# A feed-forward's second product by seven in two blocks, and a second buffer for the weights that a DMA splits

## The chip, the cores and the metric

The kernel runs on one core of a Trainium2 chip. The metric is device time in microseconds (us), from three runs of the kernel before: 2097.94, 2100.37 and 2103.01, median 2100.37. Beside these there is one profiled execution, from which all rows below are read. Engines are named as the profile names them: PE is the matmul engine and PEld its weight loads, DVE the vector engine, ACT the scalar engine, POOL GpSimd, SP the engine whose queue issues most of the transfers.

## The reference

One layer of an encoder, in float32, on 256 tokens of width 2048, with 256 memory tokens and a feed-forward width of 5632.

```python
def swiglu_ffn(h, w_in, w_out):
    gate, up = jnp.split(h @ w_in, 2, axis=-1)
    return (jax.nn.silu(gate) * up) @ w_out

x = x + 0.5 * swiglu_ffn(rms_norm(x, ffn1_norm), ffn1_w_in, ffn1_w_out)   # first feed-forward
h = rms_norm(x, mix_norm)
p = h @ w_mix_in                                   # conv value | conv gate | u | v
ya = silu(layer_norm(depthwise_conv31(val * sigmoid(gate))))
yb = gelu(u) * (masked w_s @ layer_norm(gelu(v)) + b_s)
x = x + concat(rms_norm(ya), rms_norm(yb)) @ w_mix_out
x = x + memory_cross_attention(rms_norm(x), rms_norm(mem))
x = x + 0.5 * swiglu_ffn(rms_norm(x), ffn2_w_in, ffn2_w_out)              # second feed-forward
return rms_norm(x, final_norm)
```

The change touches the second product (`@ w_out`) of the first feed-forward, the start of the mixer (`h @ w_mix_in`) and the first product (`@ w_in`) of the second feed-forward.

## The kernel before, in words

**Numbers in two parts.** A float32 operand is kept as a rounded part ("hi") and the remainder ("lo"). A product is three matmuls: hi by hi, hi by lo, lo by hi, all summed in PSUM. Weights come by DMA as raw tiles of 128x1024 float32 (512 KB); ACT writes hi (a cast), DVE writes lo (a subtraction). In `gemm_n` that is L115 and L116, in a feed-forward's groups L372 and L373 (`parts`). Four raw buffers are shared by the whole kernel (`wraw`), and three for the split ones (`whl`).

**A feed-forward's first product** goes over eleven groups of 512 columns of gate and up each (`group`; group 0 is in `run`). A group goes over the 16 k tiles of 128 rows in eight pairs, in the order SCSCSCCC. A pair C ("eight") is plain: two k tiles x two halves of the tokens x gate and up x three matmuls, 24 matmuls of 128x512 (`by_two`). A pair S ("seven") is done by a scheme with seven products in the place of eight, 21 matmuls (`three`): DVE first makes sums of weight blocks (L422, L423, L428, L435), and the matching sums of the token side ("forms") are made once, beforehand (`sides`). The seven products lie in all eight PSUM banks: six of the pool `ps` ("acc") and both of `pa` ("aux"). After the last S the banks of the products 1, 5, 6 and 7 are joined in SBUF, and at the group's end the banks of 2, 3, 4 and 8 are added (L492).

**Sums by DMA.** Three k tiles of each group (2, 7 and 13; two in the last) don't go through DVE. `summed` loads the raw tile, ACT writes minus hi into the place of lo and hi into its own, and a DMA issued by POOL adds the raw weights onto it (L394). The result lies in `hl_s`; the first feed-forward has a second such buffer in a place that comes free after group 0 (`x_given`), the second feed-forward has one. `summed` for the next use is issued after the matmuls of the present one.

**A feed-forward's second product** needs the result h with the features in the partitions. `turning` makes four transposes on PE into an aux bank, and the sink splits it (L123, L124). Each of the 22 turns gives two of the 44 k tiles; four turns are done in the last group. The product itself is four calls of `gemm_n`, one for each 512 output columns: 22 steps of two k tiles, 12 matmuls each, two banks. The other 18 turns are put one behind each step of the first call. The result is copied, turned back and added to x (`joins`), which also makes the mixer's input `x_hl` and its sums of squares.

**The mixer** begins with four calls of `gemm_n` on `w_mix_vg`. Two turns of the feed-forward's last block are done in the first of them. The convolution's steps wait in a list (`later`) from which `beside` takes a budgeted amount at each step of `gemm_n`. Its result `y_hl` is needed for `w_mix_out`.

**Order.** The instruction order on each engine is made by the framework's scheduler, which simulates the program as written and allots buffers and banks as they come free; each engine's queue is then in order.

## Time and profile before

| | us |
|---|---|
| median of three runs (2097.94 to 2103.01) | 2100.37 |
| the profiled execution | 2096.62 |
| its span, first to last instruction | 2094.9 |

| Engine | busy us | share of the span | instructions |
|---|---|---|---|
| PE | 2082.5 | 99% | 9786 |
| PEld | 1741.6 | 83% | 9786 |
| DVE | 1577.4 | 75% | 2217 |
| ACT | 1165.2 | 56% | 1451 |
| POOL | 67.7 | 3% | 83 |

The granted clock of PE is 0.999 of full speed over the span, that is 2.4 GHz. Matmuls are pipelined and their ends are modelled, so one matmul's duration (some 390 ns for 128x512) is not the pace at which they follow one another; that pace is read from the starts. A window's line gives the busy time of each engine in it, with the number of its instructions.

### The profile page before, as it was taken

To read this page: it belongs to the slowest core of one execution; us is meant where nothing else is said; L and a number is where in the kernel's file an instruction comes from. 1 tells how busy PE (TensorE), PEld (TensorE's weight loads), DVE (VectorE), ACT (ScalarE), POOL (GpSimd) and SP (SyncE) were. 2 spreads that over 40 slices of the span, in tenths; PEclk is the share of its full clock that TensorE was granted. 3 is DMA by queue.
4 is the path that set the end of the run, shared out by engine and by line. 5 is a ranking of instruction groups with operands and counts; after the bars stand their busy time and mean duration, and the time that the engine had idled before them with its cause. 6 is when DMAs were issued, how large, how long until landed. Compare 5 with 4: busy or idle time off the path is not lost.

```text
span 2094.9 us, 26646 instructions
## 1 busy us (share of the span) xinstructions
PE 2082.5 (99%) x9786; PEld 1741.6 (83%) x9786; DVE 1577.4 (75%) x2217; ACT 1165.2 (56%) x1451; POOL 67.7 (3%) x83
## 2 busy tenths in 40 slices
PE   9999999999999999999999999999999999999998
PEld 7888888888888888888888898888888888888886
DVE  7888888875655589888877666778888888787754
ACT  8665666554544454445665454556665666554443
POOL 0000000000000000000000000000000000000000
PEclk9999999999999999999999999999999999999999
DMA  9787778755665666555555543576777777556664
GB/s 368 241 263 246 226 228 263 228 183 169 226 189 188 216 233 198 187 180 183 182 197 188 186 157 117 200 272 218 217 248 251 241 225 246 182 163 203 195 192 152
DMA packets 122387, 442.34 MB, mean 211 GB/s; under 512 B 13584, under 2 KB 13968, under 8 KB 121872
## 3 DMA queue, kind: packets, MB, share of 16 engines
q1 hardware_dynamic: 113040, 407.08, 57.0%
q0 software_dynamic: 8640, 32.51, 8.3%
q8 instruction: 76, 1.25, 0.2%
q10 hardware_dynamic: 576, 1.06, 0.1%
q14 instruction: 55, 0.45, 0.1%
HBM read 438.49 MB, written 2.10 MB: 210 GB/s over the span
## 4 chain that ended last, share of the span: by engine, by line
PE 96%; DMA 2%; issue 1%; ACT 1%; DVE 0%; POOL 0%; SPq 0%; DVEq 0%; ACTq 0%; POOLq 0%
PE acc L192 12%; PE acc L191 12%; PE acc L190 12%; PE acc L319 9%; PE acc L321 9%; PE acc L318 9%; PE acc L144 8%; PE acc L151 4%; PE acc L307 3%; PE acc L305 3%; PE acc L306 3%; PE aux L293 1%; PE aux L307 1%; PE aux L305 1%; PE aux L306 1%
## 5 line engine op out<-in xcount | busy, mean ns | idle before, releaser
L116 DVE TENSOR_TENSOR hl<-raw,hl 128x1024 fp32r<-128x1024 f32 (+1 forms) x402 | 488.5, 1216 | 277.3 <-ACT hl L115 276.3
L115 ACT CAST hl<-raw 128x1024 fp32r<-128x1024 f32 (+1 forms) x402 | 419.6, 1045 | 477.8 <-PE acc L192 291.0
L373 DVE TENSOR_TENSOR hl<-spare,hl 128x1024 fp32r<-128x1024 f32 (+1 forms) x128 | 146.6, 1149 | 34.0 <-ACT hl L372 31.0
L372 ACT CAST hl<-spare 128x1024 fp32r<-128x1024 f32 (+1 forms) x128 | 126.2, 994 | 69.4 <-PE acc L321 25.9
L319 PE MATMUL acc<-hl,x_hl 128*128 128x512 f32 x408 | 147.7, 391 | 0.3 <-DVE hl L124 0.2
L373 DVE TENSOR_TENSOR hl<-raw,hl 128x1024 fp32r<-128x1024 f32 (+1 forms) x107 | 120.7, 1131 | 29.7 <-ACT hl L372 28.3
L372 ACT CAST hl<-raw 128x1024 fp32r<-128x1024 f32 (+1 forms) x107 | 103.5, 979 | 69.6 <-PE acc L321 26.7
L318 PE MATMUL acc<-hl,x_hl 128*128 128x512 f32 x408 | 141.8, 390 | 0.3 <-ACT hl L123 0.3
L321 PE MATMUL acc<-hl,x_hl 128*128 128x512 f32 x408 | 126.5, 389 | 0.0
L372 ACT CAST ring<-spare 128x1024 fp32r<-128x1024 f32 (+1 forms) x81 | 80.4, 997 | 58.9 <-PE acc L321 19.0
L373 DVE TENSOR_TENSOR ring<-spare,ring 128x1024 fp32r<-128x1024 f32 (+1 forms) x81 | 93.0, 1153 | 13.9 <-ACT ring L372 12.6
L191 PE MATMUL acc<-hl,m_hl 128*128 128x512 f32 x256 | 100.3, 392 | 0.0
L191 PE MATMUL acc<-hl,x_hl 128*128 128x512 f32 x256 | 100.3, 392 | 0.0
L192 PE MATMUL acc<-hl,m_hl 128*128 128x512 f32 x256 | 100.2, 391 | 0.0
L192 PE MATMUL acc<-hl,x_hl 128*128 128x512 f32 x256 | 99.8, 390 | 0.0
L319 PE MATMUL acc<-ring,x_hl 128*128 128x512 f32 x248 | 91.4, 389 | 0.0
L190 PE MATMUL acc<-hl,m_hl 128*128 128x512 f32 x256 | 91.2, 392 | 0.0
L318 PEld LDWEIGHTS acc<-hl,x_hl 128*128 128x128 f32 x408 | 76.4, 188 | 16.6 <-ACT hl L123 0.5
L319 PEld LDWEIGHTS acc<-hl,x_hl 128*128 128x128 f32 x408 | 76.2, 188 | 16.8 <-DVE hl L373 0.8
L190 PE MATMUL acc<-hl,x_hl 128*128 128x512 f32 x256 | 90.0, 391 | 0.0
L321 PEld LDWEIGHTS acc<-hl,x_hl 128*128 128x128 f32 x408 | 76.6, 188 | 16.0
L318 PE MATMUL acc<-ring,x_hl 128*128 128x512 f32 x248 | 88.8, 389 | 0.0
(362 smaller groups left out, 4974.9 us busy)
## 6 DMA issues: line engine op xcount, KB each, us to landing
spare<-in_ffn_w_in SPq DMA_DIRECT2D x195, 512.0 KB, 7.0
raw<-in_ffn_w_out SPq DMA_DIRECT2D x176, 512.0 KB, 3.5
raw<-in_ffn_w_in SPq DMA_DIRECT2D x156, 512.0 KB, 6.4
hl_s<-in_ffn_w_in POOLq DMA_DIRECT2D x44, 512.0 KB, 8.8
raw<-in_w_mix_vg SPq DMA_DIRECT2D x32, 512.0 KB, 4.5
raw<-in_w_k SPq DMA_DIRECT2D x32, 512.0 KB, 3.6
raw<-in_w_v SPq DMA_DIRECT2D x32, 512.0 KB, 4.3
raw<-in_w_mix_out SPq DMA_DIRECT2D x32, 512.0 KB, 4.6
```

Source lines behind the costliest of these rows:

```text
L115: nc.scalar.copy(out=hl[:, 0, :size], in_=raw[:, :size])
L116: newest[0] = nc.vector.tensor_tensor(out=hl[:, 1, :size], in0=raw[:, :size], in1=hl[:, 0, :size].bitcast(F32), op=ALU.subtract)
L144: nc.tensor.matmul(acc, lhsT=hi[:, k], rhs=xs[k], start=first and k == 0, stop=last and k == kk - 1, skip_group_check=True,)
L151: nc.tensor.matmul(acc[:, 0], lhsT=lo[:, k], rhs=xs[k][:, 0], start=False, stop=last and k == kk - 1, skip_group_check=True,)
L190: nc.tensor.matmul(acc[t], lhsT=x[:, 0, s], rhs=hi[:, k], start=k0 + k == 0, stop=False)
L191: nc.tensor.matmul(acc[t], lhsT=x[:, 0, s], rhs=lo[:, k], start=False, stop=False)
L192: nc.tensor.matmul(acc[t], lhsT=x[:, 1, s], rhs=hi[:, k], start=False, stop=k0 + k == nk - 1)
L318: nc.tensor.matmul(acc[t][g], lhsT=x[:, 0, s], rhs=hi[:, cols[g]], start=(t, g) in first, stop=False)
L319: nc.tensor.matmul(acc[t][g], lhsT=x[:, 0, s], rhs=lo[:, cols[g]], start=False, stop=False)
L321: nc.tensor.matmul(acc[t][g], lhsT=x[:, 1, s], rhs=hi[:, cols[g]], start=False, stop=last)
L372: self.cast = nc.scalar.copy(out=hl[:, 0, :n], in_=raw[:, :n])
L373: newest[0] = nc.vector.tensor_tensor(out=hl[:, 1, :n], in0=raw[:, :n], in1=hl[:, 0, :n].bitcast(F32), op=ALU.subtract)
```

## The change

The second product of the first feed-forward goes over two blocks of 1024 columns (`out_block`) in the place of four of 512. In each, four of the 22 pairs of k tiles (9, 12, 15 and 18) go by seven, the others plain. The first block takes the pairs in order, the second begins with 9 and takes the four early. A block uses four acc banks, and while its pairs by seven last all eight. The 18 turns are spread over the first block's first seven pairs, three a pair at first; the turns of the four pairs also make the sums of the token side (`out_sides`). The raw weights have four buffers, and two more from the seventh pair on; the split ones five. The weights are laid out anew, so that a k tile of 1024 columns is one row of 4 KB in each partition, as before.

Four turns of the result are left for the mixer. Its first two products are therefore begun together: the first halves (k tiles 0 to 7) of both, with the turns at every second step, and then the second halves.

The second feed-forward gets a second buffer for sums by DMA (`pair`). It lies where the results of the last two groups (h9, h10) will be, and its raw tile where h8 will be. Up to group 7 the uses alternate between the two buffers; from group 8 on there is one.

```diff
+OUT_S = (9, 12, 15, 18)
+OUT_STEPS = (
+    list(range(KF // 2)),
+    [9, 0, 1, 12, 2, 3, 15, 4, 5, 18, 6, 7, 8, 10, 11, 13, 14, 16, 17, 19, 20, 21],
+)
...
-    def gemm_n(w, x_hl, per=0.0, between=None, after=4):
-        acc = [ps.tile([P, 2, 256], F32, name="acc").rearrange("p a b -> p (a b)") for _ in range(2)]
+    def gemm_n(w, x_hl, per=0.0, between=None, after=4, acc=None, ks=None, step=2):
+        acc = acc or [ps.tile([P, 2, 256], F32, name="acc").rearrange("p a b -> p (a b)") for _ in range(2)]
         nk = w.shape[1]
-        for k0 in range(0, nk, 2):
+        for k0 in ks or range(0, nk, 2):
...
-            if between and k0 >= after:
+            if between and k0 >= after and k0 % step == 0:
...
+            self.high_pool, self.pair = high, pair
+            if pair:
+                second = high.tile([P, 2, 1024], F32R, name="hl_s2", tag="pair")
+                self.h += [high.tile([P, 2, G], F32, name="h8"), None, None]
+                high.tile([P, 120], F32, name="to_512")
+            else:
+                self.h += [high.tile([P, 2, G], F32, name=f"h{j}") for j in range(8, NG)]
...
+            if pair:
+                self.hls.append(second)
+                self.raws_summed.append(self.h[8].rearrange("p a b -> p (a b)"))
...
-            nc.sync.dma_start(out=raw, in_=self.w_in[j, :, k])
+            nc.sync.dma_start(out=raw, in_=self.w_in[j, :, k] if j < NG else self.w_out[j - NG, :, k])
             return raw
+        def buffer(self, at):
+            return at % 2 if not self.pair or self.sums_at[at][0] < 8 else 0
+        def following(self, at):
+            same = [i for i in range(at + 1, len(self.sums_at)) if self.buffer(i) == self.buffer(at)]
+            return same[0] if same else None
...
-            raw, hl = self.raws_summed[at % len(self.hls)], self.hls[at % len(self.hls)]
+            raw, hl = self.raws_summed[self.buffer(at)], self.hls[self.buffer(at)]
...
+            form = self.forms[self.spairs.index(p)] if j < NG else self.out_forms[OUT_S.index(p)]
...
+                if between is not None and k % 2 == 1:
+                    between()
...
+        def banks(self, b, names):
+            for name in names:
+                b[name] = bank(pa if name in "67" else ps, "aux" if name in "67" else "acc")
...
+            if self.pair and j == NG - 2:
+                both = self.high_pool.tile([P, 2, 2, G], F32, name="h_pair", tag="pair")
+                self.h[NG - 2:] = [both[:, i] for i in range(2)]
...
+        def out_block(self, n, result, hook, between=None):
+            b = {}
+            self.begun = set()
+            steps = OUT_STEPS[n]
+            for i, p in enumerate(steps):
+                if p in OUT_S:
+                    if "5" not in b:
+                        self.banks(b, "57612348" if i == 0 else "5761")
+                    done = all(q not in OUT_S for q in steps[i + 1:])
+                    self.seven(NG + n, p, b, done)
+                    if done:
+                        o = result()
+                        places = [o[:, t, g * G:(g + 1) * G] for g in range(2) for t in range(2)]
+                        self.joins_sevens(b, *places)
+                else:
+                    if i == 0:
+                        self.banks(b, "2348")
+                    self.eight(NG + n, p, b, i == len(steps) - 1, False, between)
+                hook(i)
+            for acc, i in (("2", 0), ("3", 2), ("4", 1), ("8", 3)):
+                nc.vector.tensor_tensor(out=places[i], in0=places[i], in1=b[acc], op=ALU.add)
+            return o
+        def out_sides(self, form, tp):
+            f1, f2 = ev.tile([P, T], F32, name="tu"), ev.tile([P, T], F32, name="tg")
+            second = ev.tile([P, T], F32, name="sq")
+            nc.scalar.copy(out=second.rearrange("p (k t) -> p k t", k=2), in_=tp[:, :, P:])
+            a11, a21, a12, a22 = tp[:, 0, :P], second[:, :P], tp[:, 1, :P], second[:, P:]
+            f = [f1[:, :P], f1[:, P:], f2[:, :P], f2[:, P:]]
+            nc.vector.scalar_tensor_tensor(out=f[0], in0=a21, scalar=-1.0, in1=a22, op0=ALU.mult, op1=ALU.subtract)
+            nc.vector.scalar_tensor_tensor(out=f[1], in0=f[0], scalar=-1.0, in1=a11, op0=ALU.mult, op1=ALU.subtract)
+            nc.vector.tensor_tensor(out=f[2], in0=a11, in1=a21, op=ALU.subtract)
+            nc.vector.tensor_tensor(out=f[3], in0=a12, in1=f[1], op=ALU.subtract)
+            for i, both in enumerate((f1, f2)):
+                s = slice(2 * i, 2 * i + 2)
+                split(form[:, s, 0], form[:, s, 1], both.rearrange("p (f n) -> p f n", f=2))
...
+            if len(self.hls) > 1:
                 self.summed(1)
...
+                    if self.out_forms is not None and i in OUT_S:
+                        self.out_sides(self.out_forms[OUT_S.index(i)], tp)
...
-        for n in range(4):
-            acc = gemm_n(a["ffn1_w_out"][n], ff.of, per=0.8 if n else 0.0, between=turns, after=0 if n == 0 else 4)
-            if n == 0:
-                pool = stack.enter_context(ff.late)
-                pool = stack.enter_context(tc.tile_pool(name="ffn1", bufs=1, reuse_waits="tile"))
-            o = pool.tile([P, 2, G], F32, name="o", bufs=2)
-            for t in range(2):
-                nc.scalar.copy(out=o[:, t], in_=acc[t])
-            turns += [turning(o, 2 * i * P, joins(4 * n + 2 * i)) for i in range(2)]
-        ff.high.close()
+        ff.ring, ff.raws = [], []
+        def next_turn():
+            if turns:
+                turns.pop(0)()
+        def turns_first(i):
+            if i == 0:
+                more = big.tile([P, 4, 2, 1024], F32R, name="more_out", tag="S2")
+                ff.ring += [more[:, q] for q in range(2)]
+                forms = more[:, 2:].rearrange("p a two n -> p (a two n)")
+                ff.out_forms = [
+                    forms[:, q * 1024:(q + 1) * 1024].rearrange("p (f two n) -> p f two n", two=2, n=P) for q in range(4)
+                ]
+            for _ in range(2 if i < 4 else 1):
+                next_turn()
+            if i == 6:
+                stack.enter_context(ff.late)
+                ff.high.close()
+                pool = rest["pool"] = stack.enter_context(tc.tile_pool(name="ffn1", bufs=1, reuse_waits="tile"))
+                ff.sums = pool.tile([P, 1024], F32, name="sums_out")
+                ff.raws += [pool.tile([P, 1024], F32, name=f"raw_out{q}") for q in range(2)]
+        def result():
+            return rest["pool"].tile([P, 2, 2 * G], F32, name="o", bufs=2)
+        def turned(o, n):
+            return [turning(o, 2 * i * P, joins(8 * n + 2 * i)) for i in range(4)]
+        o = ff.out_block(0, result, turns_first, next_turn)
+        turns += turned(o, 0)
+        def beside_second(i):
+            if i == OUT_STEPS[1].index(OUT_S[-1]):
+                ff.ring = []
+                rest["x_hl"] = gained_tile("S2")
+            elif i > 9:
+                beside(1.4)
+                if i % 2 == 0 and turns:
+                    turns.pop(0)()
+        o = ff.out_block(1, result, beside_second)
+        turns += turned(o, 1)
+        x_hl = rest["x_hl"]
...
+            accs = []
+            for n in range(2):
                 load_gate(n)
                 later.appendleft((1.6, memory_parts(n)))
-                acc = gemm_n(a["w_mix_vg"][n], lambda k: x_hl[:, k], per=1.35, between=turns, after=2)
+                accs.append(gemm_n(
+                    a["w_mix_vg"][n], lambda k: x_hl[:, k], per=1.35, between=turns, after=0, ks=range(0, 8, 2), step=4
+                ))
+            for n in range(NCT // 2):
+                if n < 2:
+                    acc = gemm_n(a["w_mix_vg"][n], lambda k: x_hl[:, k], per=1.35, between=turns, acc=accs[n], ks=range(8, KD, 2))
+                else:
+                    load_gate(n)
+                    later.appendleft((1.6, memory_parts(n)))
+                    acc = gemm_n(a["w_mix_vg"][n], lambda k: x_hl[:, k], per=1.35, between=turns, after=2)
...
+        ff = FeedForward(stack, ("S0", "S1", "S2"), x_hl, lambda k: col("ffn2_norm", k), a["ffn2_w_in"], PATTERNS[1], SUMMED[1], pair=True)
...
-    a["ffn1_w_out"] = _tiled(g["ffn1_w_out"][0], 512)
+    w = g["ffn1_w_out"][0].reshape(KF // 2, 2, P, 2, 2, 512)
+    w = np.stack([w[:, 0, :, :, ::-1], w[:, 1]], axis=1).reshape(KF, P, 2, 1024)
+    a["ffn1_w_out"] = np.ascontiguousarray(w.transpose(2, 1, 0, 3))
```

## Rows read from the trace of the kernel before

**Rows 1.** the page: its span and the busy time of each engine.

```profile
span 2094.9 us, 26646 instructions
PE 2082.5 (99%) x9786; PEld 1741.6 (83%) x9786; DVE 1577.4 (75%) x2217; ACT 1165.2 (56%) x1451; POOL 67.7 (3%) x83
```

**Rows 2.** waits of PE: engine, line, releaser: us in total, times, longest.

```profile
PE acc L319 <- DMA hl_s<-in_ffn_w_in: 0.9, 1, 0.9
```

**Rows 3.** windows (us; busy us and count of each engine; clock; DMA share; GB/s).

```profile
50.00:450.00 400.00, 400.00 (x1768) 331.10 (x1767) 328.54 (x395) 244.95 (x271) 25.48 (x30) 1.00 0.76 237
550.00:715.00 165.00, 165.00 (x739) 136.57 (x738) 86.31 (x97) 76.77 (x95) 0.00 (x0) 1.00 0.61 195
1505.00:1547.00 42.00, 41.06 (x182) 33.67 (x181) 33.66 (x42) 25.21 (x28) 2.63 (x3) 1.00 0.75 232
1547.00:1713.00 166.00, 165.97 (x733) 137.15 (x732) 137.12 (x165) 103.91 (x113) 10.46 (x12) 1.00 0.77 241
1713.00:1822.00 109.00, 109.00 (x482) 89.99 (x481) 89.03 (x106) 66.36 (x72) 6.12 (x7) 1.00 0.71 219
```

**Rows 4.** timeline of PEld (start, us, engine, line, tiles), two steps of `gemm_n`.

```profile
696.16 0.41 PEld L190 LDWEIGHTS acc<-hl,hB 128*128 128x128 f32 x2
...
715.21 0.41 PEld L190 LDWEIGHTS acc<-hl,hC 128*128 128x128 f32 x2
```

**Rows 5.** timeline of PEld in the second feed-forward: its waits for `hl_s`.

```profile
1507.77 0.30 PEld L319 LDWEIGHTS acc<-hl_s,x_hl 128*128 128x128 f32 x2 [1.36 <-DMA hl_s<-in_ffn_w_in]
...
1549.57 0.30 PEld L319 LDWEIGHTS acc<-hl_s,x_hl 128*128 128x128 f32 x2 [0.45 <-DMA hl_s<-in_ffn_w_in]
...
1715.70 0.30 PEld L319 LDWEIGHTS acc<-hl_s,x_hl 128*128 128x128 f32 x2 [0.34 <-DMA hl_s<-in_ffn_w_in]
```

**Rows 6.** DMA issues (count, KB, median us to landing), and landing of `hl_s` (min/median/max).

```profile
raw<-in_ffn_w_out SPq DMA_DIRECT2D x176, 512.0 KB, 3.5
hl_s<-in_ffn_w_in POOLq DMA_DIRECT2D x44, 512.0 KB, 8.8
...
DMA to landing us min/median/max: 5.2/8.8/9.9
```

**Rows 7.** DVE by line (xcount: min/median/max ns; or busy us, mean ns).

```profile
L408 DVE TENSOR_TENSOR spare<-spare x6: 282/284/287, 6.0 to 1384.7; 128x128 f32<-128x128 f32 x6
L422 DVE TENSOR_TENSOR spare<-raw x34: 679/683/695, 41.8 to 1800.2; 128x512 f32<-128x512 f32 x34
L492 DVE TENSOR_TENSOR spare<-spare,acc x80: 676/679/690, 90.4 to 1839.0; 128x512 f32<-128x512 f32 x80
...
L373 DVE TENSOR_TENSOR hl<-raw,hl 128x1024 fp32r<-128x1024 f32 x89 | 108.3, 1220 | 12.3 <-ACT hl L372 10.9
```

**Rows 8.** timeline at a group's end in the second feed-forward (DVE and PE).

```profile
1500.92 2.47 DVE L492 TENSOR_TENSOR spare<-spare,acc 128x512 f32<-128x512 f32 x4
...
1501.68 0.61 PE L321 MATMUL acc<-ring,x_hl 128*128 128x512 f32 x2
...
1502.13 0.39 PE L305 MATMUL acc<-ring 128*128 128x512 f32 x1
```

**Rows 9.** what a turn costs: eight loads (timeline), then DVE by line.

```profile
508.27 1.02 PEld L293 LDWEIGHTS aux<-ident,h 128*128 128x128 f32 x8
...
L124 DVE TENSOR_TENSOR hA<-aux,hA x16: 679/687/692, 460.4 to 1862.3; 128x512 fp32r<-128x512 f32 x16
L637 DVE SCALAR_TENSOR_TENSOR xT<-aux,xT x8: 683/691/692, 541.8 to 726.0; 128x512 f32<-128x512 f32 x8
L269 DVE SCALAR_TENSOR_TENSOR x_hl<-xT,pv,x_hl x48: 472/478/480, 544.1 to 1380.1; 128x256 fp32r<-128x256 f32 x48
```

**Rows 10.** waits of DVE's first sum of a pair (us in total, times, longest).

```profile
DVE spare L422 <- DMA raw<-in_ffn_w_in: 20.0, 11, 2.8
```

**Rows 11.** who writes and first reads `y_hl` (first and last start, us).

```profile
L144 PEld LDWEIGHTS acc<-y_hl,hl x256: 187/188/192, 1080.6 to 1169.5; 128*128 128x128 f32 x128
...
L124 DVE TENSOR_TENSOR y_hl<-tg,y_hl x16: 410/417/419, 1039.3 to 1069.7; 128x256 fp32r<-128x256 f32 x16
```

More of the change, by code (lines that the diff above doesn't have):

```diff
@@ L410, in sides, with x, half, begins @@
             split(self.forms[i][:, :, 0], self.forms[i][:, :, 1], f)
-        def x(self, k, t):
+        def x(self, j, k):
+            return self.x_hl[:, k] if j < NG else self.of(k)
+        def half(self, j, k, t):
             s = slice(t * P, (t + 1) * P)
-            return self.x_hl[:, k, 0, s], self.x_hl[:, k, 1, s]
-        def seven(self, j, p, b, first, last):
+            x = self.x(j, k)
+            return x[:, 0, s], x[:, 1, s]
+        def begins(self, name):
+            first = name not in self.begun
+            self.begun.add(name)
+            return first
+        def seven(self, j, p, b, last):
             k = 2 * p
```

66 lines of the change are left out of this document (32 added, 34 removed).

## The prediction

> **What bounds the kernel now.** I read the page first, for who is busy: PE 99%, beside it weight loads (PEld) 83% and DVE 75% [rows 1]. The ends of matmuls are modelled, so 99% alone does not say that PE is full, and I asked next what PE waits for: outside the launch and the attention stage one wait is left, 0.9 us for `hl_s` [rows 2]. Third come the windows by stage. PEld is busy for 331.10 of 400 us in the first feed-forward's groups and for 136.57 of 165 us in its second product: 82.8% both times, although DVE is at 82% in the one and 52% in the other [rows 3]. So 82.8% is what PEld shows while PE runs through: every product of 128x512 has one load, and they come evenly. Fourth, the period of one product: between the loads at 696.16 and 715.21 lie seven steps of `gemm_n` with 12 products each, 84 products in 19.05 us or 0.2268 us each [rows 4]. The time is a count of products times that, plus the few places where PEld falls under 82.8%. A change gains only by taking away products or such a place, and loses only by making new ones.
>
> **Products taken away.** A pair of k tiles costs the second product 12 products for each of four blocks of 512 columns, 48 in all, and 22 pairs make 1056. Now a plain pair costs 24 for each of two blocks of 1024 columns, again 48; a pair by seven costs 7 x 3 = 21 a block, 42. Four pairs (9, 12, 15, 18) save 6 each: 24 products. The transposes stay as many as they were. At 0.2268 us, and all of it on the path because PE runs through in this stage [rows 3, 4], that is 5.44 us. Bounds: nothing lower is shown, since no row has a product of this shape at another period.
> The Trainium skill (TensorE: Matmul & The Clock Gate, section "Wait — 56ns, not 53.3ns?") puts one product at its columns over 2.4 GHz plus 2.5 ns, 215.7 ns for 512 columns. By that the 24 would give 5.18 us, an estimate from the page; the rows here have 226.8 ns, with a load of its own before each product, and the measurement decides.
>
> **The second buffer for sums.** In the second feed-forward PEld falls under 82.8% in three places, each one a wait for `hl_s`: idle for 1.36, 0.45 and 0.34 us before 1507.77, 1549.57 and 1715.70 [rows 5]. By the windows these cost (34.78 - 33.67) / 0.828 = 1.34, (137.45 - 137.15) / 0.828 = 0.36 and (90.25 - 89.99) / 0.828 = 0.31 us [rows 3]. Each is the first use in a group (k = 2) after the last use in the group before (k = 13). Between the two lie k = 14, 15 and one pair by seven, 45 products or 10.2 us, and the one buffer must in that time be filled by two ACT instructions and then a DMA of 5.2 to 9.9 us [rows 6]. With two buffers in groups 1 to 7 each filling has another use's time more, so the first two waits go: 1.70 us. The third is at the start of group 8, where one buffer is left again; I let it stand. Bounds: 0, if the wait only moves to the two groups with one buffer, and 2.01, if all three go. The first feed-forward has two such buffers and shows 82.8% over 400 us [rows 3], so I take 1.70. The extra load at the start is one transfer on SP's queue and one on POOL's, ahead of need by a group.
>
> **The rhythm by seven.** A pair by seven costs DVE four additions or subtractions of 0.68, three splits of 1.22 and half a split, 0.69 by estimate [rows 7, 9]: 7.07 us in 4.76 us of PE. Two plain pairs follow with 4 x 1.22 = 4.88 us of DVE in 10.88. Together 11.95 of 15.64 us, 76%. The groups run at 82% with PE full [rows 3]: cost 0. The joins add 16 DVE additions of 0.68, 10.9 us, and take eight ACT copies away; they lie in the three plain pairs at a block's end and cost 0 there for the same reason. If that cover were gone, the price is that of the ends of blocks below.
>
> **Turns and sides.** The 18 turns left now fall into the first seven pairs, three a pair at first. Such a pair gives PE 24 x 0.2268 plus 12 transposes of about 0.12 (eight loads in 1.02 us) [rows 9], 6.9 us; DVE has 2 x 1.22 + 3 x 0.69 = 4.5. Four turns also make the sides for their pair on DVE: 4 x 0.28 [rows 7] and two half-width splits of about 0.42, between the 0.28 and the 0.69 of the neighbouring widths, 2.0 us. 6.5 of 6.9: it fits once, not twice in a row. What is scarce is the two aux banks: a side keeps its bank until its last subtraction, and behind a transpose that waits for a bank stand all later products on PE. Bounds: 0, and 4 x 2.0 = 8 us if PE stood for every side.
>
> **The ends of blocks.** The first block needs four banks at once where two did, and two of them are still read by group 10's final additions. At a group's end four such additions take 2.47 us in a row, and the next group's first product starts 0.45 us after the last one of the old [rows 8], that is at the pace of two products. In the first block the second token half is wanted six products, 1.36 us, after the start, when two of four additions are done. The same holds from the first block to the second. Bounds: 0, and 2.47 us for each of the two ends. The new buffers for raw weights lie on h8 to h10, so their transfers wait on SP's queue for the last turn, and the next weight transfers behind them; a transfer takes 3.5 us to land [rows 6] and two k tiles in hand last 5.4, so 0 here.
>
> **Into the mixer.** Four turns are left after the last block instead of two. The first halves of the mixer's first two products, 8 steps or 21.8 us, run before their features are wanted. Until then DVE has four additions (2.7), eight splits (9.8) and, for four turns, 0.69 + 4 x 0.48 each [rows 9], 10.4 us with the squares' additions set at the same 0.48. That is 22.9 us, but the last feature is wanted three steps later still, at 30 us: 0, and a step, 2.7 us, if the first turn came that late. The convolution's first input comes three steps, 8.2 us, later than before; `y_hl` is complete at 1069.7 + 0.4 and first read at 1080.6 [rows 11], so 2.3 us of cover are left: 0.
>
> **The sum.** For sides and ends together I take 1.0 us of new standstill: the ten seams inside the first feed-forward's windows cost 0 [rows 3], the row nearest to the ends, and something is left for what no row shows, four banks wanted at once and a bank held by a side. The profiled execution took 2096.62 us (span 2094.9 and 1.7 around it): 2096.62 - 5.44 - 1.70 + 1.0 = 2090.5, 6.1 less. The median of the runs shown is 2100.37, 3.75 above the profiled one, so I predict 2100.37 - 6.1 = 2094.3.
>
> **Rivals.**
> A. The second buffer brings nothing. The filling hangs on the POOL queue, whose transfers land after 5.2 to 9.9 us [rows 6], and a wait that is late for another reason than the buffer stays. Then 2096.62 - 5.44 + 1.0 = 2092.2, on the median's scale 2095.9. Against it: the first feed-forward's groups use the same queue and lose nothing.
> The Trainium skill (SBUF — State Buffer, the paragraph on the "DVE blocks DMA" trap) says that descriptors of transfers issued by GpSimd are held up while VectorE runs an instruction that takes the port both share. By that rule the landing would follow DVE's load, and the same DVE load stays after the change, which is this rival; the spread from 5.2 to 9.9 us leaves room for it.
> B. The ends and the sides eat the gain: two ends at 2.47 and half of the sides' 8 us, 8.9 us in place of the 1.0. Then 2096.62 - 7.14 + 8.9 = 2098.4, 2102.1 by the median; with the ends alone 2094.4 and 2098.2. For it: PE is in order, and no row has four banks wanted at once. Against it: [rows 8].
> C. Slower, by hunger for raw weights. The blocks have four, later six buffers for raw weights, the groups of the feed-forwards seven or eight, and a pair by seven holds two. Even in the groups DVE's first sum waited 11 times for its transfer, 20.0 / 11 = 1.8 us each [rows 10]. If all eight pairs by seven waited so and it reached PE, 8 x 1.8 = 14.5 us: 2105.0, by the median 2108.8. It decides from 6.1 / 8 = 0.8 us a pair. Against it: in the groups these waits reach PE nowhere, and six buffers last 15.6 us here, of which landing takes 3.5 and the split chain 7.1.
>
> **How the numbers follow.** The forecast gets 0.66, A 0.12, B 0.13, C 0.09. A measurement of this kernel tells about 0.2%, 4.2 us, from no change: the three runs lie 5.07 us apart. The forecast's 6.1 us are 0.29%, and with that scatter about one in eight such results would fall within 0.2%; A's 4.4 us are an even case, B mostly within, C mostly slower. Faster 0.66, same 0.23, slower 0.11. The lower end is every bound at its best, 7.45 less, or 2092.9, and half the scatter below it that a median of runs may still show, with a rest for the runs' own level: 2089. The upper end takes in A and B with its ends, to no change: 2100.5.
>
> **What would show it.** Right: PE with 24 products fewer, 9762; PEld at 82.8% from the end of group 10 to the mixer; no wait for `hl_s` in groups 2 to 7. Wrong in its steps: a gap of PE where a block begins (ends), before a transpose (sides), before L305's products with DVE's first sum waiting for a transfer (C), or waits for the sums' buffers that are as long as before (A). The forecast fails as a whole if PEld falls under 82% over the second product.

## The result, and the profile after

The changed kernel takes 2102.55 us (median of 22 runs, 2101.28 to 2103.72), the kernel before 2099.32 (22 runs beside them, 2097.94 to 2103.02): ratio 1.0014, 95% interval 1.0009 to 1.0020. It is 3.2 us slower; 6.1 us less was forecast. Between the two profiled executions the difference is 7.0 us (2103.62 against 2096.62), since the profiled one of before was faster than all its timed runs. The parts below are read from the profiles, the whole from the medians.

The page of the kernel after (span, busy time of each engine), to set beside [rows 1]:

```profile
span 2101.9 us, 26735 instructions
PE 2082.5 (99%) x9762; PEld 1740.6 (83%) x9762; DVE 1624.2 (77%) x2305; ACT 1179.0 (56%) x1473; POOL 67.7 (3%) x83
```

PE has 24 products fewer and is busy just as long. Where the time went is found by a point that both kernels pass, the first load of `m_hl` in the mixer (count, then min/median/max ns, first and last start in us), first before, then after:

```profile
L190 PEld LDWEIGHTS acc<-hl,m_hl x256: 187/188/193, 851.8 to 1080.0; 128*128 128x128 f32 x128
```

```profile
L198 PEld LDWEIGHTS acc<-hl,m_hl x256: 187/188/192, 857.6 to 1087.5; 128*128 128x128 f32 x128
```

So 5.8 of the 7.0 us are lost by then. One profile is not exact to the microsecond here: in two runs below whose work up to this point is that of the kernel before, the load stands at 852.8 and 853.6. The windows of the second product (columns as in [rows 3]) show where. The kernel before:

```profile
467.00:510.00 43.00, 43.00 (x218) 35.94 (x217) 27.36 (x32) 23.12 (x30) 0.00 (x0) 1.00 0.54 171
510.00:520.00 10.00, 10.00 (x50) 8.37 (x49) 6.12 (x8) 4.45 (x6) 0.00 (x0) 1.00 0.51 161
520.00:530.00 10.00, 10.00 (x51) 8.35 (x50) 5.52 (x7) 5.75 (x10) 0.00 (x0) 1.00 0.51 159
```

The kernel after, the same stretches, and then the middle of the hole, as the stretch from 510 to 530 is called below, in steps of 2 us:

```profile
467.00:510.00 43.00, 43.00 (x218) 35.98 (x216) 30.56 (x45) 23.93 (x34) 0.00 (x0) 1.00 0.52 171
510.00:520.00 10.00, 5.55 (x32) 4.17 (x29) 8.08 (x20) 5.59 (x13) 0.00 (x0) 0.87 0.44 161
520.00:530.00 10.00, 8.42 (x25) 6.69 (x26) 7.07 (x8) 4.56 (x5) 0.00 (x0) 0.62 0.32 106
...
550.00:715.00 165.00, 165.00 (x739) 136.59 (x738) 120.00 (x149) 89.07 (x114) 0.00 (x0) 1.00 0.63 207
...
516.00:518.00 2.00, 0.21 (x3) 0.01 (x1) 1.53 (x6) 1.26 (x3) 0.00 (x0) 0.86 0.05 18
518.00:520.00 2.00, 1.96 (x8) 1.55 (x8) 1.73 (x5) 1.00 (x3) 0.00 (x0) 0.50 0.00 0
...
522.00:524.00 2.00, 2.00 (x6) 1.52 (x6) 2.00 (x3) 1.05 (x2) 0.00 (x0) 0.50 0.17 41
...
528.00:530.00 2.00, 2.00 (x11) 1.65 (x10) 1.23 (x1) 0.19 (x1) 0.00 (x0) 1.00 0.01 4
```

Everywhere but from 510 to 530 PEld is as busy as before (82.8%, or 83.6 to 83.7% where transposes stand among the products). In these 20 us it starts 55 loads in the place of 99, and the granted clock, 1.00 until the products thin out, is 0.50 for some 10 us, about 517.4 to 527.7 (half of full speed, the lower of the two levels; (1 - 0.87) x 10 / 0.5 and (1 - 0.62) x 10 / 0.5 of the two windows). From 467 to 715 PEld has 200.0 of 248 us, 80.6%: by the prediction's own last sign, under 82% over the second product, the forecast failed. The timeline of PE in the hole (start, duration; in brackets the idle time before it and what ended it):

```profile
511.24 0.60 PE L301 MATMUL aux<-ident,h 128*128 128x128 f32 x4
513.49 1.09 PE L301 MATMUL aux<-ident,h 128*128 128x128 f32 x8 [1.65 <-DVE hB L132]
515.54 0.66 PE L301 MATMUL aux<-ident,h 128*128 128x128 f32 x4 [0.97 <-DVE hB L132]
517.99 1.97 PE L301 MATMUL aux<-ident,h 128*128 128x128 f32 x8 [1.79 <-DVE hC L132]
521.58 2.07 PE L326 MATMUL acc<-hl,hA 128*128 128x512 f32 x4 [1.62 <-ACT hl L392]
```

From 511.24 on six turns stand one behind another with no product between them, with three waits for the aux bank that DVE reads, and the next product waits for a weight cast. ACT shows why:

```profile
508.29 1.05 ACT L392 CAST more_out<-raw 128x1024 fp32r<-128x1024 f32 x1 [1.66 <-issue]
...
520.00 0.59 ACT L131 CAST hC<-aux 128x512 fp32r<-128x512 f32 x1 [0.27 <-PE aux L301]
520.48 1.05 ACT L392 CAST hl<-raw_out 128x1024 fp32r<-128x1024 f32 x1
```

Between the starts of two weight casts, 508.29 and 520.48, lie 12.2 us: ACT has the casts of seven turns (L131) and what two sides need (L574, L131) in front. PE uses one weight tile in 12 x 0.2268 = 2.72 us. The raw weights were not late here. Transfers into `raw_out` were issued at 511.00 and landed after 5.9 us at the most (issue, then what the profile says of their landing):

```profile
511.00 0.90 SPq L403 DMA_DIRECT2D raw_out<-in_ffn_w_out  x2
...
DMA to landing us min/median/max: 3.3/4.3/5.9
```

So by 517.4 they lay in SBUF, and the cast at 520.48 waited for no transfer, only for its place in ACT's queue.

The second feed-forward, windows and the waits that remain (the last two lines are PEld's timeline):

```profile
1300.00:1320.00 20.00, 18.64 (x115) 16.53 (x114) 14.29 (x25) 11.13 (x20) 0.89 (x1) 1.00 0.75 240
1505.00:1547.00 42.00, 42.00 (x187) 34.75 (x187) 34.20 (x41) 26.50 (x29) 3.15 (x4) 1.00 0.76 238
1547.00:1713.00 166.00, 166.00 (x734) 137.47 (x733) 137.31 (x164) 102.34 (x110) 9.68 (x12) 1.00 0.75 232
1713.00:1822.00 109.00, 108.20 (x476) 88.93 (x475) 88.33 (x105) 66.55 (x72) 6.29 (x8) 1.00 0.74 231
...
PEld acc L152 <- ACT hl L123: 1.2, 1, 1.2
...
1721.05 0.19 PEld L327 LDWEIGHTS acc<-hl_s,x_hl 128*128 128x128 f32 x1 [1.15 <-DMA hl_s<-in_ffn_w_in]
...
1763.81 0.30 PEld L327 LDWEIGHTS acc<-hl_s,x_hl 128*128 128x128 f32 x2 [0.49 <-DMA hl_s<-in_ffn_w_in]
```

The first two waits of [rows 5] are gone, as forecast. The third, 0.34, became 1.15, group 9 got one of 0.49, and in the attention's output product (L152, at 1312) PE waits 1.23 us for a cast, which it didn't before.

### The profile page after: what moved, and what is told of

It reads as the page before. It is cut to its first block, busy times and chain, and to the rows that moved or that the text cites. A ratio compares the mean times of both kernels' runs of the same rounds, so it can differ in the third digit from the quotient of the medians.

```text
span 2101.9 us, 26735 instructions
## 1 busy us (share of the span) xinstructions
PE 2082.5 (99%) x9762; PEld 1740.6 (83%) x9762; DVE 1624.2 (77%) x2305; ACT 1179.0 (56%) x1473; POOL 67.7 (3%) x83
## 4 chain that ended last, share of the span: by engine, by line
PE 82%; issue 13%; DMA 2%; POOL 1%; ACT 1%; DVE 1%; DVEq 0%; POOLq 0%; ACTq 0%; SPq 0%
PE acc L327 10%; PE acc L326 10%; PE acc L329 10%; PE acc L199 8%; PE acc L198 8%; PE acc L200 8%; PE acc L152 8%; PE acc L159 4%; PE acc L314 2%; PE acc L313 2%; PE acc L315 2%; PE aux L301 1%; PE aux L314 1%; PE aux L313 1%; PE aux L315 1%
## 5 line engine op out<-in xcount | busy, mean ns | idle before, releaser
L123 ACT CAST hl<-raw 128x1024 fp32r<-128x1024 f32 (+1 forms) x314 | 327.1, 1043 | 354.5 <-PE acc L200 193.3
L124 DVE TENSOR_TENSOR hl<-raw,hl 128x1024 fp32r<-128x1024 f32 (+1 forms) x314 | 380.6, 1214 | 167.3 <-ACT hl L123 165.9
L393 DVE TENSOR_TENSOR hl<-raw,hl 128x1024 fp32r<-128x1024 f32 (+1 forms) x156 | 178.8, 1149 | 57.4 <-ACT hl L392 56.1
L392 ACT CAST hl<-raw 128x1024 fp32r<-128x1024 f32 (+1 forms) x156 | 153.5, 994 | 115.1 <-PE acc L329 50.7
```

The lines of the kernel that those rows point to most:

```text
L123: nc.scalar.copy(out=hl[:, 0, :size], in_=raw[:, :size])
L124: newest[0] = nc.vector.tensor_tensor(out=hl[:, 1, :size], in0=raw[:, :size], in1=hl[:, 0, :size].bitcast(F32), op=ALU.subtract)
L392: self.cast = nc.scalar.copy(out=hl[:, 0, :n], in_=raw[:, :n])
L393: newest[0] = nc.vector.tensor_tensor(out=hl[:, 1, :n], in0=raw[:, :n], in1=hl[:, 0, :n].bitcast(F32), op=ALU.subtract)
```

## The experiments

All were timed in five rounds against the kernel before, whose median in the four groups was 2097.97, 2097.21, 2098.33 and 2097.96; ratios are to that. Between groups the ratios are compared, since this median moves by up to 2.1 us (2099.32 beside the changed kernel).

### What makes the hole: four single remedies

The trace offered four suspects: raw buffers that come free only with the last turn (W), a bank held while the sides are formed (T), the sides as such, and turns that come too fast.

**Without the two raw buffers.**

```diff
-                ff.raws += [pool.tile([P, 1024], F32, name=f"raw_out{q}") for q in range(2)]
```

> The two new buffers for raw weights are taken out: the blocks by seven load into the four old ones throughout. Theory W (the transfers into the new buffers wait for the last turns, because the buffers lie where h8 to h10 are, and the products of the eighth pair on can't run beside those turns): the standstill at 511 to 521 us and the half clock behind it go; the kernel's 2102.6 become 2092 to 2095, and PEld is at 82% in every 10 us between 470 and 700. Theory T (the turns are too many for two aux banks, above all those with sides): nothing changes here, 2101 to 2104, with the same three waits of transposes for DVE. If four buffers are too few for pairs by seven (rival C of the prediction), there are new waits of PE at 545 to 640 us and the gain is under 4.

Measured: 2100.98, ratio 1.0012 [1.0003, 1.0021]. The turns now end with products between nearly all of them, and the hole opens there and behind them, at 524 to 530 (PEld 4.56 in 520:530).

**Without sides** (the sums of the token side for the second product are left out; the forms are filled once from x).

```diff
-                        self.out_sides(self.out_forms[OUT_S.index(i)], tp)
+                        pass
...
+                nc.scalar.copy(out=forms, in_=xT.rearrange("p k t -> p (k t)"))
```

> Left out: the sums of the token side for the four pairs (their tiles are filled once from x). A turn then holds its aux bank only for its own split. Theory T: the standstill goes or falls under 3 us, 2093 to 2096. Theory W: the last turns still stand alone on PE, without sides they are shorter (by some 4 us for the two sides that lie in the standstill), so 2097 to 2100 and still over 4 us of PE idle near 511 us.

Measured: 2103.18, ratio 1.0023 [1.0014, 1.0032]; PEld 6.64 and 6.60 in 510:520 and 520:530. The sides are not needed for a hole, though it is smaller without them. The time can't be set beside the others: the one copy that fills the forms takes ACT 3.62 us at 471.82 and makes a hole of its own (PEld 3.16 and 2.50 of 5 us in 470:475 and 475:480).

**Sides from a copy in SBUF**, so that their bank is free sooner.

```diff
-            nc.scalar.copy(out=second.rearrange("p (k t) -> p k t", k=2), in_=tp[:, :, P:])
...
+            for q in range(2):
+                nc.scalar.copy(out=rows[q], in_=tp[:, q])
...
```

> ACT copies the whole turned tile to SBUF and the sides are made from there, so that the aux bank is free after the copies instead of after DVE's last subtraction. Theory T: the standstill falls by most of its length, 2094 to 2098. Theory W: only the two sides inside it get shorter, by some 2 us: 2099 to 2102.

Measured: 2100.96, ratio 1.0012 [1.0003, 1.0021]; PEld 4.16 in 510:520.

**Turns spread evenly**, two a pair.

```diff
-            for _ in range(2 if i < 4 else 1):
-                next_turn()
-            if i == 6:
+            next_turn()
+            if i == 8:
```

> The 18 turns are spread evenly, two a pair over pairs 0 to 8 in the place of three, then two; the new raw buffers come after the ninth pair. Theory W: fewer turns are left alone at the end and PE has its weights for pairs 7 and 8; the standstill falls to under 4 us: 2094 to 2098. Theory T: two turns a pair are within what the banks give, the standstill goes as well: 2092 to 2095. (It tells both from the third possibility, that the loss has nothing to do with the turns: 2101 to 2104.)

Measured: 2100.58, ratio 1.0013 [1.0005, 1.0022]. The lump of six turns is gone but for the last three, the hole is not: PEld 4.43 in 520:530.

No remedy is clear of the changed kernel's 1.0014 [1.0009, 1.0020] by its ratio, and with each a hole stays, in its place or further on; none of the theories stands alone.

### Where the sevens stand

**Late sevens**, alone and with the turns spread.

```diff
-    list(range(KF // 2)),
+    [0, 1, 2, 3, 4, 5, 6, 7, 8, 10, 11, 9, 13, 14, 12, 16, 17, 15, 19, 20, 18, 21],
```

> The same late order of the pairs by seven, but the turns as in the change, three a pair and then two. Theory Q: the last six turns stand together on PE without products, and the standstill stays at about 511 to 521 us: 2099 to 2102. If what counts is only the neighbourhood of the first seven, the gain is the same as with both: 2093 to 2095.

Measured: 2101.96, ratio 1.0022 [1.0013, 1.0031]; PEld 2.90 in 510:520.

> Two turns a pair over pairs 0 to 8, and the first pair by seven only after two more plain pairs (order 0 to 8, 10, 11, 9, 13, 14, 12, 16, 17, 15, 19, 20, 18, 21). Theory Q (near the last turns the splits of weights stand in ACT's and DVE's queues behind splits of turns, whose transposes stand in PE's queue behind products, so that the five split buffers run dry just where the first pair by seven needs its sums): with plain products between the last turn and the first seven no standstill is left, PEld at 82% from 470 to 700, 2092.5 to 2095 beside 2098.0 of the kernel before. Rival R (the pairs by seven themselves starve PE in this stage, wherever they stand): a standstill of 3 us or more stays and moves to the new first seven near 535 us, 2098 to 2101.

Measured: 2100.51, ratio 1.0012 [1.0003, 1.0021]; PEld 6.19, 6.84 and 6.30 in three windows from 520 to 550. The first run is as theory Q said, the second as rival R said. The trace of the second is that of its slowest execution, 2105.18.

**The first block by eight alone**, two turns a pair.

```diff
-                if p in OUT_S:
+                if p in OUT_S and n == 1:
...
```

> The changed kernel, but no pair of the first block by seven products (its 22 pairs by eight, 12 products more than the changed kernel, 2.7 us at 0.227), two turns in each of its first nine steps; the sides of the token side are still formed, for the second block. Theory V (the sevens close behind the turns make the standstill, since their sums and splits take DVE and ACT just when the turns' splits do): no window of 10 us between 500 and 550 has under 8 us of weight loads, the clock stays at 1.00, time 2095 to 2097. Theory Q (the turns themselves, with a split that stands in ACT's and DVE's queue in front of the weights, and few split weights ahead, whatever kind of pair follows): a standstill and a half clock remain there, time 2100 to 2104.

Measured: 2102.17, ratio 1.0018 [1.0009, 1.0027]. Theory V has fallen, and R as the cause of this hole: without any seven near the turns there is a hole of 4 us. Q's range is met. Its trace shows two causes at once, ACT first, then PE, then SP's queue:

```profile
519.47 0.59 ACT L131 CAST hB<-aux 128x512 fp32r<-128x512 f32 x1 [3.99 <-PE aux L301]
...
530.74 1.05 ACT L392 CAST hl<-raw_out 128x1024 fp32r<-128x1024 f32 x1 [2.23 <-DMA raw_out<-in_ffn_w_out]
```

```profile
518.84 1.03 PE L301 MATMUL aux<-ident,h 128*128 128x128 f32 x8
...
526.54 1.35 PE L301 MATMUL aux<-ident,h 128*128 128x128 f32 x8
531.84 2.07 PE L326 MATMUL acc<-hl,hA 128*128 128x512 f32 x4 [3.95 <-ACT hl L392]
```

```profile
526.31 0.91 SPq L403 DMA_DIRECT2D raw_out<-in_ffn_w_out  x2
```

First, ACT stands for 3.99 us before a turn's split, whose transposes (518.84) lie in PE's queue behind 27 products; meanwhile it refills none of the tiles that PE empties. Second, the next raw weights go to `raw_out`, whose transfer is issued at 526.31, just before the last turns' transposes, and lands 4.4 us later; in the changed kernel it was issued at 511.00 and was in time.

### Rate of the turns, or the late transfer

**One turn a pair in a first block by eight.**

```diff
-        o = ff.out_block(0, result, turns_first, next_turn)
+        o = ff.out_block(0, result, turns_first)
...
-            if i == 8:
+            if i == 17:
```

> As the one before (first block by eight alone), but one turn in each pair of rows in the place of two: the last turn stands near the first block's end. Theory Q: with half as many turns in a stretch ACT and DVE keep ahead, no standstill, clock 1.00 throughout the block, and the stage costs 12 products less than before: 2094 to 2097 (before less 2.7 us, and what the second buffer costs). Theory V says the same of this kernel as of the one before, so the two differ by Q and agree by V. If both still stand still, the cause is neither rate nor kind of pair.

Measured: 2095.97, ratio 0.9989 [0.9980, 0.9999], 6.2 us under the same kernel with two turns a pair, as theory Q said. The hole is gone:

```profile
510.00:520.00 10.00, 10.00 (x48) 8.19 (x47) 5.52 (x6) 3.64 (x4) 0.00 (x0) 1.00 0.62 190
520.00:530.00 10.00, 10.00 (x49) 8.31 (x48) 6.51 (x11) 5.69 (x9) 0.00 (x0) 1.00 0.60 165
530.00:540.00 10.00, 10.00 (x49) 8.26 (x48) 5.22 (x5) 4.53 (x6) 0.00 (x0) 1.00 0.58 184
```

In both kernels `raw_out` comes in behind the last turn, here nine pairs later.

**Two turns a pair, but without `raw_out`** (the kernel by eight, with the edit of the first experiment).

> The kernel with the first block by eight and two turns a step, without the two extra buffers for raw weights that lie where the last results lie. In its trace two things stood in the hole at 527.9 to 531.8: TensorE's queue was empty, since the splits of two turns stood in ACT's queue from 515.1 to 520.0 in front of the weights, and the next weights came from transfers that were issued at 526.3, behind the last turn. Theory Q alone (splits of turns in front of weights): the hole stays, 3 to 4 us, time 2101 to 2103. Theory W alone (transfers behind the last turn): the hole goes, the clock stays at 1.00, time 2095 to 2097. Both: a hole of 1 to 2.5 us, time 2097 to 2100.

Measured: 2098.17, ratio 1.0002 [0.9994, 1.0010]: 4.0 us by the medians, 0.16% or 3.4 us by the ratios, under the kernel with `raw_out`, so the late transfer is one cause there. Its executions lie from 2094.8 to 2102.49, wider than those of any other run (the next, the late sevens with spread turns, has 6.5 us). The profiled one is the fastest of them and has no hole:

```profile
520.00:530.00 10.00, 10.00 (x49) 8.26 (x48) 7.47 (x13) 5.76 (x10) 0.00 (x0) 1.00 0.56 167
530.00:540.00 10.00, 10.00 (x47) 8.28 (x46) 5.10 (x5) 4.35 (x5) 0.00 (x0) 1.00 0.58 180
```

By the median the answer is "both", by this one trace "W"; what the slow executions look like inside was not seen. The rate can be lowered and `raw_out` kept, and the hole is gone; `raw_out` can be taken away from the changed kernel (first experiment), and it stays.

The rate alone is not the cause. The kernel before does its turns, too, two behind every 24 products (two turns are the eight transposes of a line):

```profile
502.17 1.03 PE L293 MATMUL aux<-ident,h 128*128 128x128 f32 x8
508.50 1.03 PE L293 MATMUL aux<-ident,h 128*128 128x128 f32 x8
```

It goes on like this from 489.50 to 521.17, and its trace shows no wait of PEld from 467 to 530. To the same rate the new kernels add, above all, the sides of four turns, the buffers that wait for the last turn and, in the changed kernel, the sevens behind. At one turn a pair sides and buffers make no hole. Which of them it takes at two a pair no run separates: a block by eight with two turns a pair and no sides was not tried.

### What the half clock costs

**Fourteen useless products behind the last turn** of the kernel with spread turns, where PE stood idle. They are computed and not used.

```diff
+                idle = bank(ps, "acc")
+                with tc.issue_after(turned_last[0].ins):
+                    for q in range(14):
+                        nc.tensor.matmul(idle, lhsT=ff.of(1)[:, 0, :P], rhs=..., start=q == 0, stop=q == 13)
```

> The kernel with evenly spread turns (2100.6 in its run), and 14 useless products of 128x512 behind the last turn on TensorE, some 3.1 us, in the hole of 3 us in which TensorE had no weights; they compute nothing that is used. If the half clock behind the hole comes from the hole, the granted clock stays at 1.00 from 520 to 540 and the kernel is 2 to 4 us faster than without them, 2097 to 2099, though it does more work. If the clock falls there for another reason, it falls again, and the time is 2100.6 or up to 3 us more.

Measured: 2100.34, ratio 1.0010 [1.0001, 1.0018], against 2100.58 and 1.0013 without them. Windows of the kernel with spread turns, then of the filled one:

```profile
526.00:528.00 2.00, 0.00 (x0) 0.00 (x0) 1.79 (x4) 0.65 (x2) 0.00 (x0) 0.96 0.00 0
...
532.00:534.00 2.00, 2.00 (x6) 1.55 (x5) 2.00 (x3) 1.04 (x1) 0.00 (x0) 0.50 0.79 260
```

```profile
526.00:528.00 2.00, 2.00 (x10) 1.65 (x9) 1.79 (x4) 0.64 (x2) 0.00 (x0) 1.00 0.00 0
...
532.00:534.00 2.00, 2.00 (x10) 1.52 (x9) 2.00 (x3) 0.98 (x2) 0.00 (x0) 1.00 0.89 256
...
540.00:550.00 10.00, 9.66 (x40) 6.92 (x39) 5.71 (x7) 4.30 (x5) 0.00 (x0) 1.00 0.31 117
```

Half of the expectation came: with PE kept at work the granted clock stays at 1.00, so the half clock came from the hole. The 2 to 4 us did not come. PE at full speed uses up the few weights sooner and waits again, at 540 to 550 (PEld 6.92 in the place of 8.29). The half clock lay over a time in which weights were short anyway, and its own price does not show in the time.

### The second buffer

**The buffer without the new second product**, and the changed kernel without the buffer.

```diff
-..., PATTERNS[1], SUMMED[1])
+..., PATTERNS[1], SUMMED[1], pair=True)
```

> The second buffer for sums in the second feed-forward alone; the first feed-forward's second product and the mixer as in the kernel before. By the traces so far the waits for the sums at groups 3 and 4 (1.8 us of idle) go and those at groups 8 and 9 grow to about 1.6: 0 to 1 us faster than the kernel before, 2097 to 2098. By the prediction it would be 1.7 us, 2096.3.

Measured: 2099.26, ratio 1.0008 [1.0000, 1.0017]: 1.7 us slower (0 to 3.6), not faster.

> The change without the second buffer in the second feed-forward. If the buffer brings what the prediction says, this is 1.7 us slower than the change; by the traces 0 to 1 us. The standstill near 511 us stays as it is, since nothing before the second feed-forward is touched: 2101 to 2103.

Measured: 2102.15, ratio 1.0022 [1.0014, 1.0031], the same as the changed kernel's 1.0014 within the intervals. In the first of the two the scheduler has put the second buffer's first filling into the start of `w_o` (window, then ACT's timeline):

```profile
1300.00:1310.00 10.00, 8.64 (x47) 7.33 (x46) 5.50 (x10) 5.67 (x9) 0.89 (x1) 1.00 0.74 239
...
1305.10 1.06 ACT L421 ACTIVATE hl_s<-h 128x1024 fp32r<-128x1024 f32 x1 [1.45 <-DMA h<-in_ffn_w_in]
...
1306.99 1.99 ACT L123 CAST hl<-raw 128x1024 fp32r<-128x1024 f32 x2
```

ACT waits 1.45 us for the raw tile of a group that comes 100 us later, fills for 2 us, and `w_o`'s casts stand behind it.

**The filling tied into its own stage**, and both buffers for one group more.

```diff
-                self.summed(1)
+                with tc.issue_after(self.cast.ins):
+                    self.summed(1)
...
-            return at % 2 if not self.pair or self.sums_at[at][0] < 8 else 0
+            return at % 2 if not self.pair or self.sums_at[at][0] < 9 else 0
```

> The kernel before with the second buffer for sums by DMA, as in the run of the buffer alone, but the first filling of the second buffer is tied behind a weight cast of the second feed-forward's first group, so that it can't stand in w_o's start, and both buffers serve one group longer (to group 8). Theory B1 (the buffer alone lost what its first filling cost in w_o): the wait for ACT at 1300 to 1312 is gone, the waits for the sums by DMA of 1.4, 0.5 and 0.3 us are gone but perhaps for one in the last two groups, time 1 to 2 us under before: 2095.5 to 2096.5. Theory B2 (the buffer brings nothing, its waits only move to other groups or become waits for casts): before's time within 0.5 us.

Measured: 2095.85, ratio 0.9989 [0.9980, 0.9998]. Theory B1 holds, in time and in its trace. The run has two edits in one: in the trace of the buffer alone PEld waits 1.6 us in `w_o`, which the tie takes away, and 2.2 us for the sums in two places, which the further group takes away but for 0.3.

```profile
1300.00:1310.00 10.00, 10.00 (x58) 8.70 (x57) 5.80 (x12) 5.37 (x9) 0.00 (x0) 1.00 0.75 259
...
1713.00:1822.00 109.00, 109.00 (x482) 90.07 (x481) 89.15 (x105) 64.43 (x70) 5.22 (x6) 1.00 0.67 205
```

### Put together

**Slow turns, sevens last in the first block** (two turns in each of the first four steps, then one).

```diff
-    list(range(KF // 2)),
+    [0, 1, 2, 3, 4, 5, 6, 7, 8, 10, 11, 13, 14, 16, 17, 19, 9, 12, 20, 15, 18, 21],
...
-            if i == 6:
+            if i == 13:
...
-        o = ff.out_block(0, result, turns_first, next_turn)
+        o = ff.out_block(0, result, turns_first)
```

> The changed kernel, with all its sevens in both blocks, but in the first block one turn a step behind the first four steps (the last in the fourteenth), and the four pairs by seven among the last six. If the turns' rate was what made the standstill, the 12 products less than in the kernel with slow turns and no sevens there (2095.97) count: 2.7 us, so 2093 to 2094, and no window of 10 us between 450 and 650 has under 8 us of weight loads. If sevens need more of DVE and ACT than they save on TensorE even behind the turns, a standstill appears at 580 to 620, and the time is 2096 to 2100.

Measured: 2096.56, ratio 0.9993 [0.9984, 1.0001]: the second case. The hole at the turns is gone, no window of 10 us from 500 to 570 has under 8.2 us of weight loads, and one stands behind them (6.74, 7.80 and 7.19 in three windows from 570 to 600).

> Slow turns without sevens in the first block (2095.97) and the second buffer's first filling tied into the second feed-forward (2095.85 by itself on the second product of before): if the two gains are independent they add, 2.4 and 2.5 us under before, 2093 to 2094. If one only takes waits that the other had already moved, 2095 to 2096.

Measured: 2093.71, ratio 0.9979 [0.9970, 0.9988], in the range for gains that add. That they add is not shown by it: the kernel with slow turns, from which the expectation starts, had the second buffer already, untied, with waits of 1.6 us in `w_o` and 2.4 us for the sums in its trace. The tie and the further group brought 0.10% here and 0.19% without the new second product; each difference is uncertain by some 0.13%.

> Everything that the change meant to do, with slow turns, late sevens and the filling tied: if products, rate and buffer add up, 24 products (5.4 us) and 2 us of waits less than before, some 2091; if the sevens in the first block bring nothing, as the kernel with slow turns and the tied filling, 2093 to 2094; if the late sevens stand still, 2096 or more.

Measured: 2093.49, ratio 0.9978 [0.9969, 0.9987]. It beats both kernels, by 4.5 us the one before and, over the two comparisons, by 0.36% or 7.6 us the changed one. But its 12 products less in the first block bring nothing beside the kernel before it in this list. Its windows, and then one of that kernel:

```profile
570.00:580.00 10.00, 8.79 (x38) 6.75 (x37) 9.90 (x13) 4.51 (x6) 0.00 (x0) 1.00 0.69 249
580.00:590.00 10.00, 9.07 (x41) 7.04 (x39) 9.00 (x12) 6.79 (x9) 0.00 (x0) 1.00 0.44 136
590.00:600.00 10.00, 10.00 (x43) 8.04 (x44) 10.00 (x14) 5.83 (x7) 0.00 (x0) 1.00 0.56 184
```

```profile
570.00:580.00 10.00, 10.00 (x47) 8.24 (x47) 3.72 (x4) 4.42 (x6) 0.00 (x0) 1.00 0.17 55
```

With the sevens close together DVE is full, 9.90 of 10 us, and PEld loses (16.56 - 13.79) / 0.828 = 3.3 us where 2.7 were saved. DVE's load is not the only candidate. Just before, SP's queue stands for 10.5 us for a raw buffer that is free only when a seven's last sum has read it (L474; total, times, longest, in 556 to 570):

```profile
SPq L403 <- DVE raw L474: 10.5, 1, 10.5
```

From 560 to 566 no transfer moves. That is the prediction's rival C, a pair by seven that holds two raw buffers; no run separates it from DVE's load. That the sevens would do better with two plain pairs between them, as in the groups, was not tried with slow turns.

## Why the prediction was wrong

**Products: right in count, not refuted in price, the gain covered up.** 9762 products, and PEld as busy as before outside the hole. From 510 to 530 PEld starts 55 loads instead of 99, and 24 instead of 20 of these belong to transposes: 48 products fewer. By 550 five are made good, since no turns are left, so 43, or 9.8 us, are lost and 5.4 gained: 4.4 of the 5.8 us at `m_hl`. The other 1.4 are in no one place, and the two profiles at 852.8 and 853.6 say that a profile can be off by as much; 0.6 stood already at the stage's start. Without a hole the price fits: between the tied buffer alone and the tied buffer with slow turns and sevens in the second block alone lie 0.10%, 2.1 us give or take 2.7, where 12 products are 2.7. By the traces the three kernels with the old second product reach `m_hl` at 851.8, 852.8 and 853.6, the two with 12 products less and slow turns at 850.1 and 850.4, 2.5 us earlier on the average.

**Turns and sides: the step that failed**, 1.0 us taken for this and the ends, about 10 measured. The step added up DVE's load in one pair, 6.5 of 6.9 us, and asked whether it fits. Neither DVE (8.08 and 7.07 of 10 us) nor ACT (5.59 and 4.56) was full over the hole, and the forecast's own upper bound of 8 us, PE standing for every side, was too low. What I had not worked out is the order: a turn is a round trip from PE to ACT and DVE and back to PE's banks, through three queues in order, and what stands behind it on ACT and DVE are the weights that PE needs next. In the changed kernel the last six turns, two of them with sides, stood together, and PE, ACT and DVE waited for one another in turn, each partly idle, with raw weights landed and uncast. Without sides the kernel before passes turns at two a pair with no wait; with sides and the new buffers, two a pair left a hole and one a pair none. Which of the additions is the least that makes the hole stays open.

**Raw weights on h8 to h10, set at 0.** I named the wait on SP's queue and covered it with "two k tiles in hand". In the changed kernel's hole the transfers were in time, issued at 511.00 against a cast at 520.48; that the last turns stand together there is tied to these buffers all the same, since without them products lie between the turns (first experiment). In the kernel by eight the transfer itself was late, at 526.31, and there were no k tiles in hand, since the turns had kept ACT from casting: the cover was used up by the very stretch that made the wait. Taking these buffers away gave 3.4 to 4.0 us there.

**The second buffer: 1.70 right for what it removes, wrong in all.** Groups 2 to 7 have no wait, as said. Not seen were the filling that the scheduler hoists into `w_o`, 1.2 to 1.6 us of waiting in the changed kernel and with the buffer alone, though I wrote that the extra load is "ahead of need by a group", and the single buffer behind group 8, where a wait of 0.34 became 1.15 and one of 0.49 came. Tied in place, with a group more, the buffer gave 2.3 us by the ratio, with 0.4 to 4.2 as its interval: the size forecast, and the third wait besides.

**Ends of blocks, rhythm by seven, mixer: right at 0.** The window 467:510 and the 165 us from 550 have the PEld time of before (35.98 for 35.94 us, 136.59 for 136.57), and from `m_hl` on the two kernels keep their distance until `w_o`. For the rhythm this holds where two plain pairs lie between sevens.

**The rivals.** B's time, 2102.1 by the median, is the one that came, by luck: its ends cost nothing, and its sides are not needed for a hole. C had the right kind of cause, hunger for weights, at the wrong place: ahead of the first seven, at the turns, and for split weights, not raw ones. What C describes stands in the trace with the sevens close together. A's outcome came, no gain from the buffer clear of the noise, by a filling at the wrong place and a wait at one buffer, and not by a late queue.

## What to carry to other kernels

A sum of busy times says whether work fits; it doesn't say whether it fits in order. Where one unit of work goes through several queues and back, count what stands behind it in each queue and how much finished input the bound engine has in hand at that moment, and don't use one cover twice. Work that is issued early for a later stage has to be tied to that stage, or the scheduler may put it in front of something that is needed now, as it did here with the second buffer's first filling.

## What the runs showed of the hardware

In the changed kernel and in the one with spread turns the granted clock went to 0.50 while PE stood idle and came back after some 10 and 7 us, with PE at work again; in the filled kernel it stayed at 1.00. I had expected 2 to 4 us from that. It changed the median by 0.2 us, 2100.58 to 2100.34 in two comparisons (0.03% by the ratios), and PE waited for weights further on.
